# Weight splits made a layer ahead, mean subtractions on GpSimd and an earlier LayerNorm in a two-layer decoder trunk

## The chip, the cores and the metric

The kernel runs on one core of a Trainium2 chip. The metric is the device time of one launch in microseconds, the median of several runs. The profile is of one execution, and its times count from the first instruction of that execution.

## What is computed

The trunk has two layers over 512 tokens of width 1024, all in float32. In each layer the input is RMS-normalised and multiplied by one combined input matrix, whose columns give the branch, the queries of a small attention over 256 memory rows (4 heads of 128) and a gate of width 2048. Layer one's branch is a retention with 8 heads; layer two's is a gated depthwise convolution. The branch and the attention are multiplied by silu(gate), go through an output matrix, are RMS-normalised again and added to the input. The branch of layer two is what the change is about:

```python
u, g, xq, gate = split(proj)          # 1536, 1536, 512, 2048
glu = u * sigmoid(g)
y = causal_depthwise_conv(glu, 31 taps) + dw_b
y = silu(layernorm(y, ln_g, ln_b))    # mean and variance over 1536 channels
```

## The kernel before

**Weights.** The matrices are cut into units of 256 x 512 numbers (512 KB). Each is loaded in float32 by SP (`send`, L159), cast to the matmul's type by ScalarE (`whi`, L181), and the remainder is subtracted by GpSimd in two halves (`wlo`, L188) or by VectorE for some units (L185). A product of activations and weights is then three matmuls, hi x hi, hi x lo and lo x hi (`split3`, L252 to L256). Units 0 to 7 belong to the memory keys and values, 8 to 71 to layer one, 72 on to layer two. When TensorE begins a unit, the one three units on is split (`prefetch`, L193).

**Chunks.** `weave` (L229) writes the program in order: a chunk of six large matmuls, then the side steps due at that place (attention, LayerNorm), then the hooks, then steps of VectorE's list, then products. The order is kept as written on every engine (`manual_schedule`). Layer two is the first projection (32 half chunks), the stages c1, c2, xq, c3, c4, gx, conv5, gate 0, gate 1, gate 2 of 16 chunks each, and the output projection of 64. Per chunk RATE says how many list steps follow and OFFLOAD how many products; what is left over adds up to at most 2.

**The convolution.** The 1536 channels are 12 tiles of 128 x 512, summed in pairs. The list (`tap_sums`, L1084) holds one VectorE multiply-add per tap and tile (`tap_sum`, L1081). `product` (L1050) takes a tap off it: ScalarE multiplies (L1065), GpSimd adds (L1066), only for the pair after the one being summed, once that pair's input tiles are there.

**The LayerNorm.** Once four pairs are summed, LN[0] chunks later, a first mean over eight tiles is taken (`m0_mean`, L1160). It is subtracted from each tile (`shift`, L1151, L1153); the result is squared by ScalarE (L1157) and the squares are added by GpSimd (`gather`, L1131). These moments stand in a second list, `behind`, which every second step serves. `ln_ready` (L1223) empties both lists and treats the last two tiles; `ln_sums` (L1232) lets TensorE sum the squares and the remaining mean; `ln_cols` and `ln_spread` give the inverse deviation. `z_norm` and `z_gate` (L1266, L1274) finish each tile on VectorE and ScalarE and split it for the output projection. LN[1] to LN[4] are the places of these steps, counted from the start of gate 2; the output projection starts at 16.

**The attention** runs beside conv5 and gate 0, by XA: scores (TensorE, VectorE's maxima L505, the negated and scaled maxima L507), exponentials and probabilities (ScalarE, L516, L528), transposes (`p_T`, evacuated by ScalarE at L539 into one of two PSUM buffers' successors), and `av` (L541): TensorE multiplies, VectorE multiplies by the gate (L549), ScalarE casts (L551); two places later VectorE takes the remainder (`yx_lo`, L555).

Of the kernel before, what the change touches and what calls it, by code (L numbers as in the profile page):

```python
# [19 lines left out]
P = 128  # L20
# [71 lines left out]
def trunk(ctx, tc, x, x_t, mem_t, pos, g_cols, w_mem, post_g, w0, w1, dw_w, dw_b,  # L92
# [48 lines left out]
    nc.gpsimd.dma_start(out=inv, in_=c_inv)  # L141
    nc.gpsimd.dma_start(out=zeta, in_=c_zeta)
    nc.gpsimd.dma_start(out=taps, in_=dw_w.rearrange("p (c k) -> p c k", c=NB))
    for i, v in enumerate((dw_b, ln_g, ln_b)):
        nc.gpsimd.dma_start(out=cvec[:, i, :], in_=v)
# [14 lines left out]
    def send(upto):  # L160

        for i in range(sent["dma"], min(upto, sent["conv"] + 3, nu)):
            raws[i] = gp.tile([P, 2, G], F32, tag="wraw", bufs=3, name=nm("wraw"))
# [3 lines left out]
            sent["dma"] = i + 1  # L167

    def conv_units(upto):
        for i in range(sent["conv"], min(upto, nu)):  # L170
            send(i + 1)
            hi = gp.tile([P, 2, G], F32R, tag="whi", bufs=5, name=nm("whi"))
            lo = gp.tile([P, 2, G], F32R, tag="wlo", bufs=5, name=nm("wlo"))
            raw = raws.pop(i)
# [15 lines left out]
            his[i], los[i] = hi, lo  # L190
            sent["conv"] = i + 1
# [276 lines left out]
    def evac_v(a, acc):  # L468
# [9 lines left out]
           (7, conv(4)), (8, lambda: squares("m", mt)), (11, conv(5)), (13, conv(6)),  # L478
# [11 lines left out]
    def xattn(xq, gx, yx, rs=None):  # L490
# [3 lines left out]
        def scores(t):  # L494
            mx, nb = tiny([P, XH]), tiny([P, XH])
            scs = []
            for hp in range(2):
                sc = tp_ps()
                scs.append(sc)
                for j in range(2):  # L500
# [6 lines left out]
                nc.vector.tensor_scalar(out=nb[:, hs], in0=mx[:, hs], scalar1=-1.0,  # L507
                                        scalar2=rs[:, t:t + 1] if rs is not None else SCALE,
                                        op0=ALU.mult, op1=ALU.mult)
            pes[t] = scs, nb  # L510

        def exps(t):
            scs, nb = pes[t]
            pe, sm = w4([P, XH, M]), tiny([P, XH])
            for h in range(XH):
# [25 lines left out]
        def av(t):  # L541
# [9 lines left out]
            nc.scalar.copy(out=yx[0][:, :, tok], in_=g)  # L551
# [157 lines left out]
    with tc.tile_pool(name="l0", bufs=1) as lp:  # L709
# [99 lines left out]
        def x_rstd():  # L809
            rx["c"] = col_rstd([0, 1])  # L810
            rx["s"] = tiny([P, NT])
            nc.gpsimd.tensor_scalar(out=rx["s"], in0=rx["c"], scalar1=SCALE, scalar2=0.0,
                                    op0=ALU.mult, op1=ALU.add)
# [12 lines left out]
        def evac_gx(a, acc):  # L826
# [8 lines left out]
                 (5, x_rstd), (5, mem_diags), (7, x_diags)] + [(c, steps(2)) for c in range(4, 8)])  # L835
        weave(proj(hT, False, evac_copy(xq)), [(0, mem_spread), (1, x_spread)]
# [4 lines left out]
        xa = xattn(xq, gx, yx, rx["s"])({0: (1, 7, 11), 1: (9, 15, 19), 2: (17, 23, 27), 3: (25, 31, 34)})  # L841
# [175 lines left out]
        hT = nxt["get"]  # L1017

# [3 lines left out]
    with tc.tile_pool(name="l1", bufs=1) as lp:  # L1022
# [243 lines left out]
        def z_norm(ct):  # L1266
# [3 lines left out]
            nc.vector.tensor_tensor(out=z, in0=z, in1=ln["rb"], op=ALU.mult)  # L1270
            nc.scalar.activation(out=z, in_=z, func=AF.Silu, scale=cvec[:, 1, ct:ct + 1],
                                 bias=cvec[:, 2, ct:ct + 1])

        def z_gate(ct):  # L1274
            c, j = ct // 4, ct % 4
            z = cy[:, ct, :]
            nc.vector.tensor_tensor(out=z, in0=z, in1=gates[c][j], op=ALU.mult)  # L1277
            if ct in (0, 4):
# [9 lines left out]
        def z_step(ct):  # L1288
            if ct < NB:
                z_norm(ct)  # L1290
            if ct:
                z_gate(ct - 1)

        gate(0, part_of(xa, 1), R[7])
        gate(1, part_of(xa, 2), R[8])
        def norm_of(a, b):

            return [(pos_ - a, fn) for pos_, fn in
                    [(LN[1], ln_ready), (LN[2], ln_sums), (LN[3], ln_cols), (LN[4], ln_spread)]
                    + [(LN[4] + (i + 1) // 2, lambda i=i: z_step(i)) for i in range(NB + 1)]  # L1300
                    if a <= pos_ < b]

        gate(2, norm_of(0, 16), R[9])
# [4 lines left out]
        def yT1(j):  # L1308
            if j >= 4:
# [4 lines left out]
                 norm_of(16, 99))  # L1314
# [65 lines left out]
```

## Time and profile before

| | before |
|---|---|
| median of 3 runs | 830.45 us (830.06 to 831.77) |
| profiled execution: own time, span | 831.9 us, 829.8 us |
| TensorE, VectorE, ScalarE, GpSimd busy | 97%, 63%, 42%, 50% of the span |
| mean granted TensorE clock | 0.99 |
| DMA | 84.97 MB, 102 GB/s over the span |

The span runs from the first to the last instruction of the program; the execution's own time is some 2 us longer. TensorE's busy time is that of pipelined matmuls, so a stretch in which it is busy throughout need not be one at full pace; the number of matmuls in a stretch tells that. DMA-issuing instructions count as idle.

### The profile page before, as it was taken

What the parts mean: (1) busy time and instruction counts of PE and PEld (TensorE: products, weight loads), DVE (VectorE), ACT (ScalarE), POOL (GpSimd) and SP (SyncE); (2) the same over time, 40 slices, a digit from 0 to 9 for tenths busy, and PEclk for the clock granted to TensorE, in tenths of its full rate; (3) what the DMA queues carried; (4) which work ended last, traced back from release to release, by engine and by line L of the source; (5) the groups of instructions that cost most, each with busy time, mean ns of one, the idle gap of its engine ahead of it and who ended that gap; (6) DMA issues with size and microseconds to landing.
All of it is one profiled execution on the core that took longest, in us unless ns stands there. A gap on an engine that the chain in (4) does not pass through costs nothing.

```text
span 829.8 us, 10432 instructions
## 1 busy us (share of the span) xinstructions
PE 806.1 (97%) x3904; PEld 674.9 (81%) x3904; DVE 520.1 (63%) x824; ACT 347.8 (42%) x559; POOL 417.5 (50%) x381
## 2 busy tenths in 40 slices
PE   8999999999999999999999999999999989998896
PEld 7778888888888888888888988888877878766686
DVE  5798112124664641343326489999999999979523
ACT  5754256521111122333325425544578654245511
POOL 3144433346747644100024168998987798356101
PEclk9999999999999999999999999999999999999899
DMA  7733221231222222233522242322312113311612
GB/s 254 267 109 102 102 76 52 77 115 67 74 88 68 73 77 102 87 116 102 203 101 91 89 152 77 103 101 86 106 66 75 51 51 130 121 54 51 226 54 101
DMA packets 24961, 84.97 MB, mean 102 GB/s; under 512 B 2976, under 2 KB 4512, under 8 KB 24656
## 3 DMA queue, kind: packets, MB, share of 16 engines
q1 hardware_dynamic: 24256, 83.90, 29.1%
q8 instruction: 30, 0.49, 0.2%
q10 hardware_dynamic: 432, 0.21, 0.1%
q0 software_dynamic: 224, 0.21, 0.1%
q14 instruction: 19, 0.16, 0.1%
HBM read 80.11 MB, written 4.19 MB: 102 GB/s over the span
## 4 chain that ended last, share of the span: by engine, by line
PE 76%; DVE 14%; ACT 4%; DMA 3%; POOL 1%; issue 1%; SPq 0%; POOLq 0%; DVEq 0%; ACTq 0%
PE mm L254 22%; PE mm L255 22%; PE mm L256 22%; DVE acc L1081 5%; DMA wraw<-in_w_mem 2%; DVE cy L1277 2%; PE acc L921 1%; DVE wlo L185 1%; ACT whi L181 1%; PE tp L545 1%; PE tp L502 1%; DVE cy L1153 1%; PE tp L902 1%; PE acc L923 1%; DVE cy L1270 1%
## 5 line engine op out<-in xcount | busy, mean ns | idle before, releaser
L188 POOL TENSOR_TENSOR wlo<-wraw,whi 128x512 fp32r<-128x512 f32 x184 | 239.1, 1324 | 234.0 <-ACT whi L181 225.1
L254 PE MATMUL mm<-big,whi 128*128 128x512 f32 (+1 forms) x608 | 235.7, 388 | 5.3 <-ACT whi L177 2.6
L256 PE MATMUL mm<-big,wlo 128*128 128x512 f32 (+1 forms) x608 | 228.3, 375 | 0.4 <-DVE wlo L185 0.3
L255 PE MATMUL mm<-big,whi 128*128 128x512 f32 (+1 forms) x608 | 227.9, 375 | 0.0
L1081 DVE SCALAR_TENSOR_TENSOR acc<-gl,taps,acc 128x512 f32<-128x512 f32 x292 | 195.7, 747 | 0.4
L181 ACT CAST whi<-wraw 128x1024 fp32r<-128x1024 f32 x133 | 137.2, 1046 | 88.7 <-PE mm L256 32.7
L256 PE MATMUL mm<-whi,big 128*128 128x512 f32 (+1 forms) x432 | 168.3, 390 | 0.6 <-POOL big L701 0.5
L254 PE MATMUL mm<-whi,big 128*128 128x512 f32 (+1 forms) x408 | 162.6, 398 | 0.0
L255 PE MATMUL mm<-wlo,big 128*128 128x512 f32 (+1 forms) x408 | 157.8, 387 | 0.9 <-DVE wlo L185 0.9
L254 PEld LDWEIGHTS mm<-big,whi 128*128 128x128 f32 x608 | 115.7, 190 | 25.3 <-ACT big L1220 2.8
L256 PEld LDWEIGHTS mm<-big,wlo 128*128 128x128 f32 x608 | 115.5, 190 | 21.5 <-DVE wlo L185 0.5
L255 PEld LDWEIGHTS mm<-big,whi 128*128 128x128 f32 x608 | 115.7, 190 | 18.9 <-issue 0.5
L256 PEld LDWEIGHTS mm<-whi,big 128*128 128x128 f32 x432 | 81.7, 189 | 19.0 <-POOL big L701 2.2
L255 PEld LDWEIGHTS mm<-wlo,big 128*128 128x128 f32 x408 | 76.8, 188 | 16.0 <-DVE wlo L185 1.3
L254 PEld LDWEIGHTS mm<-whi,big 128*128 128x128 f32 x408 | 76.7, 188 | 14.5 <-issue 0.2
L185 DVE TENSOR_TENSOR wlo<-wraw,whi 128x1024 fp32r<-128x1024 f32 x41 | 53.3, 1316 | 41.2 <-ACT whi L181 41.1
L1066 POOL TENSOR_TENSOR part<-part,pr 128x512 f32<-128x512 f32 x56 | 72.6, 1317 | 5.6 <-ACT pr L1065 5.6
L894 ACT ACTIVATE kz<-tp,zeta 128x384 f32<-128x384 f32 x8 | 4.7, 584 | 96.5 <-PE tp L892 96.5
L1065 ACT ACTIVATE pr<-gl,taps 128x512 f32<-128x512 f32 x56 | 38.3, 716 | 0.1
L505 DVE TENSOR_REDUCE tiny<-tp 128x2 f32<-128x512 f32 x16 | 11.0, 684 | 27.0 <-PE tp L502 27.0
L327 POOL TENSOR_SCALAR tiny<-tiny,tiny 128x1 f32<-128x1 f32 x11 | 3.0, 271 | 41.1 <-ACT pr L602 34.6
L1039 ACT ACTIVATE gl<-mm 128x512 f32<-128x512 f32 x12 | 7.2, 599 | 38.5 <-PE mm L256 38.5
(220 smaller groups left out, 885.6 us busy)
## 6 DMA issues: line engine op xcount, KB each, us to landing
wraw<-in_w SPq DMA_DIRECT2D x126, 512.0 KB, 3.3
wraw<-in_w_mem SPq DMA_DIRECT2D x7, 512.0 KB, 5.3
big<-in_x_t SPq DMA_DIRECT2D x2, 1024.0 KB, 7.4
o<-in_x SPq DMA_DIRECT2D x1, 2048.0 KB, 8.7
x1d<-o SPq DMA_DIRECT2D x4, 512.0 KB, 2.7
o<-x1d SPq DMA_DIRECT2D x1, 2048.0 KB, 10.0
out<-o SPq DMA_DIRECT2D x3, 512.0 KB, 2.6
big<-in_mem_t SPq DMA_DIRECT2D x4, 256.0 KB, 7.2
```

The source lines that it names most:

```text
L181: nc.scalar.copy(out=hi, in_=raw)
L185: nc.vector.tensor_tensor(out=lo, in0=raw, in1=hi.bitcast(F32), op=ALU.subtract)
L188: nc.gpsimd.tensor_tensor(out=lo[:, k], in0=raw[:, k], in1=hi[:, k].bitcast(F32), op=ALU.subtract)
L254: nc.tensor.matmul(dst, lh, rh, start=start, stop=False)
L255: nc.tensor.matmul(dst, lh, rl, start=False, stop=False)
L256: nc.tensor.matmul(dst, ll, rh, start=False, stop=stop)
L502: nc.tensor.matmul(sc[:, j * M:(j + 1) * M], xq[:, h, t * P:(t + 1) * P], mkT[:, h, :], start=True, stop=True)
L505: nc.vector.reduce_max(out=mx[:, hs], in_=sc.rearrange("p (a b) -> p a b", a=2), axis=AX.X)
L1065: nc.scalar.activation(out=pr, in_=gl[:, k:k + S], func=AF.Copy, scale=tap)
L1066: nc.gpsimd.tensor_tensor(out=parts[ct], in0=parts[ct], in1=pr, op=ALU.add)
L1081: nc.vector.scalar_tensor_tensor(out=o, in0=gl[:, k:k + S], scalar=tap, in1=ac, op0=ALU.mult, op1=ALU.add)
L1277: nc.vector.tensor_tensor(out=z, in0=z, in1=gates[c][j], op=ALU.mult)
```

## The change

- Eighteen units of layer two (76 to 110, every other one) are split during layer one, half a unit at every sixth chunk: load 256 KB, cast on ScalarE, subtract on GpSimd, store both parts to DRAM. In layer two the two parts are loaded.
- The first-mean subtractions of tiles 0 to 9 go to GpSimd.
- OFFLOAD rises; the LayerNorm steps move forward from the start of the output projection to that of gate 2 (LN counts from gate 0 now), and a tile's steps are spread, two chunks a tile, with its split not before the second chunk of the output projection.
- In the attention the negated maxima are made on ScalarE, and the cast L551 becomes a step of its own one place later.
- Six small constant loads move from GpSimd's queue to SP's, into the first projection.

```diff
-OFFLOAD = (0, 0.3, 0.6, 0.6, 0.6, 0.5, 0.6, 0.9, 0.5, 0, 0.5)
-LN = (7, 17, 19, 21, 24)
+OFFLOAD = (0, 0.4, 0.8, 0.8, 0.8, 0.8, 0.8, 0.9, 0.8, 0.4, 0.5)
+LN = (7, 32, 34, 36, 39)
+PRE = range(76, 112, 2)
...
-    nc.gpsimd.dma_start(out=inv, in_=c_inv)
...
+    def load_small():
+        nc.sync.dma_start(out=inv, in_=c_inv)
+        nc.sync.dma_start(out=zeta, in_=c_zeta)
...
     def conv_units(upto):
...
+            if i in PRE:
+                nc.sync.dma_start(out=hi.bitcast(F32), in_=ahead[i][:, :, 1])
+                nc.sync.dma_start(out=lo.bitcast(F32), in_=ahead[i][:, :, 0])
+                continue
...
+        for n in range(len(todo)):
+            if n:
+                store(n - 1)
+            load(n + 1)
+            st = stage[n]
+            nc.scalar.copy(out=st[:, 1].bitcast(F32R), in_=st[:, 0])
+            nc.gpsimd.tensor_tensor(out=st[:, 0], in0=st[:, 0], in1=st[:, 1], op=ALU.subtract)
+            yield
+        store(len(todo) - 1)
+
+    pace = {"every": 6, "n": 0}
...
-           (7, conv(4)), (8, lambda: squares("m", mt)), (11, conv(5)), (13, conv(6)),
+           (7, conv(4)), (8, lambda: squares("m", mt)), (9, load_small), (11, conv(5)), (13, conv(6)),
...
-                nc.vector.tensor_scalar(out=nb[:, hs], in0=mx[:, hs], scalar1=-1.0,
...
         def exps(t):
...
+            nc.scalar.activation(out=nb, in_=mx, func=AF.Copy,
+                                 scale=rsn[:, t:t + 1] if rs is not None else -SCALE)
...
-            nc.scalar.copy(out=yx[0][:, :, tok], in_=g)
+
+        def yx_hi(t):
+            tok = slice(t * P, (t + 1) * P)
+            nc.scalar.copy(out=yx[0][:, :, tok], in_=gx[:, :, tok])
...
-                        (p, p_T, t, 0.7), (a, av, t, 1.3), (a + 2, yx_lo, t, 0.0)]
+                        (p, p_T, t, 0.7), (a, av, t, 1.3), (a + 1, yx_hi, t, 0.0),
+                        (a + 2, yx_lo, t, 0.0)]
...
+        pace["steps"] = split_ahead(lp)
+        hooks.append(ahead_hook)
...
         def shift(ct):
             z = cy[:, ct, :]
-            nc.vector.tensor_tensor(out=z, in0=z, in1=ln["m0s"], op=ALU.subtract)
+            eng = nc.gpsimd if ct < NB - 2 else nc.vector
+            eng.tensor_tensor(out=z, in0=z, in1=ln["m0s"], op=ALU.subtract)
...
-                    [(LN[1], ln_ready), (LN[2], ln_sums), (LN[3], ln_cols), (LN[4], ln_spread)]
-                    + [(LN[4] + (i + 1) // 2, lambda i=i: z_step(i)) for i in range(NB + 1)]
...
+            steps_ = [(LN[1], ln_ready), (LN[2], ln_sums), (LN[3], ln_cols), (LN[4], ln_spread)]
+            for i in range(NB):
+                at = LN[4] + 1 + 2 * i
+                steps_ += [(at + n, lambda f=f, i=i: f(i)) for n, f in enumerate((z_norm, z_act, z_gate))]
+                steps_.append((max(49 + i, at + 3), lambda i=i: z_split(i)))
+            return [(pos_ - a, fn) for pos_, fn in sorted(steps_, key=lambda s: s[0]) if a <= pos_ < b]
+
+        gate(0, part_of(xa, 1) + norm_of(0, 16), R[7])
+        gate(1, part_of(xa, 2) + norm_of(16, 32), R[8])
+        gate(2, norm_of(32, 48), R[9])
...
+    nc = bacc.Bacc("TRN2", target_bir_lowering=False, num_devices=1,
+                   dynamic_dma_scratch_size=2048)
```

## Rows read from the trace of the kernel before

**Rows 1.** Page, engines: busy us, share of the span, instructions.

```profile
PE 806.1 (97%) x3904; PEld 674.9 (81%) x3904; DVE 520.1 (63%) x824; ACT 347.8 (42%) x559; POOL 417.5 (50%) x381
```

**Rows 2.** Windows, 20 us: PE, PEld, DVE, ACT, POOL busy (x), clock, DMA.

```profile
540.00:560.00 20.00, 20.00 (x90) 16.54 (x89) 19.69 (x31) 9.90 (x14) 20.00 (x17) 1.00 0.29 105
740.00:760.00 20.00, 19.41 (x84) 15.09 (x83) 19.76 (x24) 12.71 (x19) 16.41 (x12) 1.00 0.13 42
760.00:780.00 20.00, 15.11 (x54) 11.47 (x53) 13.91 (x13) 9.68 (x12) 5.98 (x5) 0.83 0.34 112
```

**Rows 3.** Windows by stage: layer one, conv5, gate 0, gate 2; columns likewise.

```profile
60.00:320.00 260.00, 260.00 (x1281) 221.46 (x1280) 112.68 (x244) 82.28 (x134) 137.17 (x118) 1.00 0.24 81
...
604.90:639.90 35.00, 33.26 (x162) 27.28 (x161) 34.72 (x58) 27.71 (x60) 28.59 (x25) 1.00 0.22 76
639.90:673.60 33.70, 30.69 (x163) 25.03 (x161) 33.55 (x49) 24.89 (x44) 25.65 (x18) 1.00 0.14 47
...
697.10:718.90 21.80, 21.80 (x98) 18.02 (x97) 21.80 (x34) 6.48 (x8) 11.41 (x10) 1.00 0.47 167
```

**Rows 4.** Sources: form: ns min/median/max; who sat idle for whom.

```profile
L1153 DVE TENSOR_TENSOR cy<-cy,m x12: 680/1118/1773, 652.4 to 722.5; 128x512 f32<-128x512 f32 x12
...
L1131 POOL TENSOR_TENSOR sum<-sum,pr x8: 1266/1462/1740, 657.9 to 688.3; 128x512 f32<-128x512 f32 x8
...
L1066 POOL TENSOR_TENSOR part<-part,pr x56: 1275/1293/1755, 502.6 to 679.7; 128x512 f32<-128x512 f32 x56
...
  DVE cy L1153: 16.7, 10
```

**Rows 5.** Groups: busy us, mean ns; taps, and GpSimd's weight halves.

```profile
L1081 DVE SCALAR_TENSOR_TENSOR acc<-gl,taps,acc 128x512 f32<-128x512 f32 x292 | 195.7, 747 | 0.4
...
L1081 DVE SCALAR_TENSOR_TENSOR cy<-gl,taps,acc 128x512 f32<-128x512 f32 x12 | 8.4, 739 | 0.0
...
L188 POOL TENSOR_TENSOR wlo<-wraw,whi 128x512 fp32r<-128x512 f32 x184 | 239.1, 1324 | 234.0 <-ACT whi L181 225.1 <-issue 8.8
```

**Rows 6.** Timeline of ScalarE: gate 0's first chunks (start, length).

```profile
645.88 1.04 ACT L181 CAST whi<-wraw 128x1024 fp32r<-128x1024 f32 x1
646.82 1.06 ACT L539 COPY w<-tp 128x512 f32<-128x512 f32 x2
647.77 1.71 ACT L528 ACTIVATE w<-w,tiny 128x256 f32<-128x256 f32 x4
...
650.00 0.58 ACT L1164 ACTIVATE m<-tp 128x512 f32<-128x512 f32 x1
...
653.28 0.64 ACT L1157 ACTIVATE pr<-cy 128x512 f32<-128x512 f32 x1
```

**Rows 7.** Page, DMA issue (us to landing); timeline, one SP issue.

```profile
wraw<-in_w SPq DMA_DIRECT2D x126, 512.0 KB, 3.3
...
2.11 0.43 SPq L399 DMA_DIRECT2D big<-in_mem_t  x1
```

**Rows 8.** Timeline of VectorE, 642 to 652 us.

```profile
642.33 0.17 DVE L507 TENSOR_SCALAR tiny<-tiny 128x2 f32<-128x2 f32 x1
...
647.04 4.67 DVE L1081 SCALAR_TENSOR_TENSOR acc<-gl,taps,acc 128x512 f32<-128x512 f32 x7
651.79 0.69 DVE L549 TENSOR_TENSOR big<-tp,big 128x512 f32<-128x512 f32 x1
```

**Rows 9.** Timeline of TensorE: the chunk behind the variance sums.

```profile
727.65 0.80 PE L254 MATMUL mm<-whi,big 128*128 128x512 f32 x1
```

**Rows 10.** Windows: the stop at 766; first and last of three behind it.

```profile
766.00:768.00 2.00, 0.00 (x0) 0.00 (x0) 1.19 (x2) 1.57 (x4) 0.72 (x2) 1.00 0.00 0
770.00:772.00 2.00, 1.05 (x3) 0.86 (x4) 2.00 (x3) 0.68 (x1) 0.00 (x0) 0.50 0.04 8
...
774.00:776.00 2.00, 2.00 (x6) 1.52 (x6) 0.00 (x0) 0.49 (x1) 0.00 (x0) 0.50 1.00 252
```

More of the change, by code (lines that the diff above doesn't have):

```diff
@@ L140, in trunk @@
     nc.gpsimd.memset(mean_of, 1.0 / BW)
-    nc.gpsimd.dma_start(out=inv, in_=c_inv)
[L142 to L145, printed above, removed]
+    def load_small():
+        nc.sync.dma_start(out=inv, in_=c_inv)
+        nc.sync.dma_start(out=zeta, in_=c_zeta)
+        nc.sync.dma_start(out=taps, in_=dw_w.rearrange("p (c k) -> p c k", c=NB))
+        for i, v in enumerate((dw_b, ln_g, ln_b)):
+            nc.sync.dma_start(out=cvec[:, i, :], in_=v)
     units = [w_mem[i] for i in range(8)]
@@ L173, in conv_units @@
             lo = gp.tile([P, 2, G], F32R, tag="wlo", bufs=5, name=nm("wlo"))
+            his[i], los[i] = hi, lo
+            sent["conv"] = i + 1
+            if i in PRE:
+                nc.sync.dma_start(out=hi.bitcast(F32), in_=ahead[i][:, :, 1])
+                nc.sync.dma_start(out=lo.bitcast(F32), in_=ahead[i][:, :, 0])
+                continue
             raw = raws.pop(i)
@@ L189, in conv_units, with split_ahead, load, store @@
                                             in1=hi[:, k].bitcast(F32), op=ALU.subtract)
-            his[i], los[i] = hi, lo
-            sent["conv"] = i + 1
+    ahead = {i: dp.tile([P, 2, 2, G], F32, name=f"ahead{i}") for i in PRE}
+    def split_ahead(pool):
+        todo = [(i, k) for i in PRE for k in range(2)]
+        stage = {}
+        def load(n):
+            if n < len(todo):
+                i, k = todo[n]
+                stage[n] = pool.tile([P, 2, G], F32, tag="stage", bufs=3, name=nm("stage"))
+                nc.sync.dma_start(out=stage[n][:, 0], in_=units[i][:, k * G:(k + 1) * G])
+        def store(n):
+            i, k = todo[n]
+            nc.sync.dma_start(out=ahead[i][:, k], in_=stage.pop(n))
+        load(0)
+        yield
[6 more added lines that the diff above has]
+            nc.gpsimd.tensor_tensor(out=st[:, 0], in0=st[:, 0], in1=st[:, 1], op=ALU.subtract)
+            yield
+        store(len(todo) - 1)
+    pace = {"every": 6, "n": 0}
+    def ahead_hook():
+        pace["n"] += 1
+        if pace["n"] >= pace["every"]:
+            pace["n"] = 0
+            next(pace["steps"], None)
     def prefetch():
@@ L506, in scores @@
                                      axis=AX.X)
-                nc.vector.tensor_scalar(out=nb[:, hs], in0=mx[:, hs], scalar1=-1.0,
-                                        scalar2=rs[:, t:t + 1] if rs is not None else SCALE,
-                                        op0=ALU.mult, op1=ALU.mult)
-            pes[t] = scs, nb
+            pes[t] = scs, mx, nb
         def exps(t):
-            scs, nb = pes[t]
+            scs, mx, nb = pes[t]
             pe, sm = w4([P, XH, M]), tiny([P, XH])
+            nc.scalar.activation(out=nb, in_=mx, func=AF.Copy,
+                                 scale=rsn[:, t:t + 1] if rs is not None else -SCALE)
             for h in range(XH):
@@ L810, in x_rstd @@
             rx["c"] = col_rstd([0, 1])
-            rx["s"] = tiny([P, NT])
-            nc.gpsimd.tensor_scalar(out=rx["s"], in0=rx["c"], scalar1=SCALE, scalar2=0.0,
-                                    op0=ALU.mult, op1=ALU.add)
+            for key, sc in (("s", SCALE), ("sn", -SCALE)):
+                rx[key] = tiny([P, NT])
+                nc.gpsimd.tensor_scalar(out=rx[key], in0=rx["c"], scalar1=sc, scalar2=0.0,
+                                        op0=ALU.mult, op1=ALU.add)
             for t, acc in late_v:
@@ L1017, in trunk @@
         hT = nxt["get"]
+        hooks.clear()
+        for _ in pace["steps"]:
+            pass
     with tc.tile_pool(name="l1", bufs=1) as lp:
@@ L1277, in z_gate, with z_split @@
             nc.vector.tensor_tensor(out=z, in0=z, in1=gates[c][j], op=ALU.mult)
+        def z_split(ct):
+            c, j = ct // 4, ct % 4
+            z = cy[:, ct, :]
             if ct in (0, 4):
```

21 lines of the change are left out of this document (6 added, 15 removed).

## The prediction

> **What bounds the kernel now.** I read the engines' busy times first. TensorE is busy 97% of the span, VectorE 63%, GpSimd 50% [rows 1]; the sum of the matmuls is fixed by the work, so only the 24 us in which TensorE stands, and the stretches in which it runs slowly, can be won. The windows say where they lie. At full pace 20 us hold 90 large matmuls, as 540 to 560 us does; 740 to 760 holds 84 and 760 to 780 only 54, at a mean granted clock of 0.83 [rows 2]. Those 42 missing matmuls are worth 42 x 0.227 = 9.5 us (0.227 us is a sixth of a chunk, below). The stages come next: layer one from 60 to 320 us has no stop at all, gate 0 of layer two takes 33.7 us with TensorE busy 30.7, and the undisturbed gate 2 takes 21.8 us for its 16 chunks, that is 1.36 us a chunk and 0.227 a matmul [rows 3]. In every one of the gate stages VectorE is busy without a break. So layer two's second half is a race between TensorE and VectorE's list of taps, subtractions and LayerNorm steps, and the change rearranges that list. Each engine works its instructions strictly in the order in which they are written: in gate 0 ScalarE's squares sit behind VectorE's mean subtractions for 16.7 us in all [rows 4].
>
> **Counting the written order.** I number layer two's chunks from 1: 32 half chunks of the first projection, then 16 a stage, so gate 0 is 145 to 160, gate 1 161 to 176, gate 2 177 to 192, the output projection 193 to 256. Working the pace rule (RATE and OFFLOAD added per chunk, products only for the pair of tiles after the one being summed) through for the kernel before gives 304 multiply-adds and 56 products, as the rows have [rows 4, 5]. With the new numbers it gives 290 and 70: the sum of OFFLOAD x 16 rises by 30, but products wait for tiles that are not there yet, and only 14 more are issued. The mean of the first eight tiles then comes after chunk 145 instead of 148; the ten subtractions fall at 145 (one), 146 (two), 147 (one), 149 (three), 150 (one) and 158, 159 (the two late ones); and at the new place of ln_ready, chunk 177, twelve taps are still unspent and are poured out at once.
>
> **Parts with little in them.** The 36 half units in layer one cost ScalarE 36 x 0.53 = 19 us (two copies take 1.06 [rows 6]) and GpSimd 36 x 1.3 = 47 us over some 390 us. From 60 to 320 us ScalarE is busy 82 of 260 us and GpSimd 137 [rows 3], and an eviction is wanted three chunks (4.1 us) after it is issued; I take 0. A gain is excluded where TensorE never stands; if every copy held an eviction it would be 19 us. In layer two 18 units lose a cast of 1.04 us and two GpSimd halves of 1.32 [rows 5, 6], 48 us of GpSimd, which pays for the products and subtractions there. Their loads are issued three units (16 us) ahead, and a 512 KB load lands in 3.3 us [rows 7]: 0. Six small loads leave GpSimd's queue for SP's, where an issue takes 0.43 us [rows 7]: between -1 (the first weights come sooner, with GpSimd's loads out of their way; an estimate of mine below the 0.43 x 6) and +2.6 us if the weights behind them wait for all six; I take 0. The negated maximum leaves VectorE (0.17 us each [rows 8]) for ScalarE, where it stands in front of exponentials that waited for VectorE anyway: 0, at most 16 x 0.17 = 2.7 us won.
>
> **The chain that I expect to decide.** Moved to GpSimd, a subtraction is followed on the same queue by the addition of its own square: subtract (GpSimd), square (ScalarE), add (GpSimd), subtract the next. Each round trip is serial, and GpSimd's queue also holds the products. The price of a GpSimd step: its product sums have a median of 1.29 us, the additions of squares 1.46, up to 1.74 [rows 4]. The long ones ran beside VectorE's subtractions, which themselves reached 1.77 us against 0.68 at best [rows 4]; with the subtractions gone from VectorE I take 1.27, and keep 1.74 as the upper end.
> The Trainium skill (GPSIMD Engine Reference, Key points) says that GpSimd shares its SBUF interfaces with VectorE and contends with instructions of two SBUF inputs; the multiply-adds read one operand from PSUM, so by that rule the low price holds, while by the median of the additions themselves the sum would come out 15 x 0.19 = 2.9 us later. The same page of the Trainium skill (Engine selection) puts two-input elementwise work on VectorE, GpSimd being about twice as slow; the trace has 0.68 at best against 1.27 here, 1.9 times.
> Step by step, on the clock of the trace of before:
> - ScalarE reaches the new place of the mean, right behind chunk 145's cast, at 646.9; its copy takes 0.6 [rows 6]: mean ready 647.5.
> - Up to subtraction 6 GpSimd does 7 subtractions, 5 additions and 3 product sums (chunks 146 to 148): 15 x 1.27 = 19.1. Five squares lie open between them, 0.64 [rows 6] and two hand-overs, 0.05 each by my estimate: 3.7. The first open square stands behind the chunk's copies and probabilities on ScalarE [rows 6]: about 2. Sum 24.8: 672.3.
> - Square 6, a product, and the copy yx_hi of token block 1 (position 5 of gate 0, now after the squares): 0.6 each, 674.2.
> - VectorE reaches yx_lo of that block, chunk 151, after the product at 651.8 [rows 8], four taps later: 655.2. It waits for yx_hi until 674.3, that is 19 us, with all its taps queued behind.
> - TensorE: the PSUM buffer of attention block 2 is freed by copies behind square 7, about 678; at 1.36 us a chunk and its attention matmuls it is there at 665. It stands some 13 us, but what it loses here it would lose later anyway.
> - VectorE's rest up to the variance sums: 67 taps and 2 copies at 0.667 (seven taps 4.67 us [rows 8]) 46.0; five attention steps at 0.69 3.5; two subtractions at 1.11 [rows 4] 2.2; two additions at 0.69 1.4. Sum 53.1: 727.4. The tenth product sum, at about 690, does not hold it further.
> - TensorE, free again at 678, is at the variance sums (three chunks into gate 2) near 714, and stands about 13 us until 727.4. The mean matmul takes 0.6: chunk 180 starts at 728.0.
>
> Now against before: there the chunk behind the variance sums starts at 727.65 [rows 9], but that is chunk 197, 17 chunks further on. So the end moves by 0.3 + 17 x 1.36 = 23.4 us. Back come the 9.5 us of the first part [rows 2]: the LayerNorm tiles (three VectorE steps each, 36 us for twelve) start some 20 chunks before they are needed, and that wait is hidden; were it not, 9.5 us come back. Against that, after the stop at 766 the granted clock was 0.50, 1.2 instead of 2.4 GHz, in the windows from 770 to 776 [rows 10], three of them: half of 6 us lost. The new long stop is nearest to that one: +3.0. Sum: 23.4 - 9.5 + 3.0 = **+16.9 us**. The profiled execution's own time is 831.9 against a median of 830.45; I add the difference to the median: **847.4 us**.
>
> **The rivals.**
> *The chain does not hold VectorE* (not slower): if the squares' round trips finished before VectorE comes to yx_lo at 655.2, everything behind moves up by the 19.1 us: 828.3, with the same bounds 826 to 833. For it: GpSimd has 48 us less splitting. Against it: 15 steps cannot be done in the 7.7 us between the mean and yx_lo; it needs the mean some 19 us earlier, and ScalarE is not free for it. The point from which it decides is a hold of 17 us: below that the kernel is no slower. Chance 0.15, of which 0.09 faster and 0.06 the same.
> *The LayerNorm tiles are late again* (slower still): they start only at about 740, and if they are as slow as the 3 us each of now and the splits queue on GpSimd, 9.5 us are not won: 856.9. Against it: first wanted at chunk 205, last at 225. Chance 0.06.
> *Layer one pays*: 36 copies hold evictions or their stores hold SP's queue: up to 19 us, 858 to 866. Against it: TensorE's unbroken 260 us there [rows 3]. Chance 0.04.
> *My chain*: 0.75. Its own range: +7.1 with GpSimd at 1.74 and +2.6 at the start, so 857; down 1.7 for TensorE's idle time in the stage before gate 0 (35.0 long, 33.3 busy [rows 3]) and 2.7 for the maxima: 843.
>
> **The numbers.** The likeliest case gives 847.4. The range 834 to 858 leaves out the unheld case and layer one's, 0.19. A measurement of this kernel can tell about 0.2% from no change, 1.7 us; faster by more 0.09, within 0.06, slower 0.85.
>
> **What would show it.** Right: 290 multiply-adds, 70 products; VectorE idle near 655 to 674 waiting for ScalarE's yx copy; ScalarE's squares waiting for GpSimd; TensorE standing over 10 us at attention block 2 in gate 0 and again at the variance sums in gate 2; no stop among the LayerNorm tiles; layer one as before. Wrong: if VectorE runs through gate 0 without that hole, or if the variance sums come before 715.

## The result, and the profile after

The changed kernel takes **853.15 us** (median of 4 runs, 852.90 to 853.39) against 830.97 us for the kernel before, measured beside it (4 runs, 830.06 to 831.77): a ratio of 1.0267, 95% interval 1.0249 to 1.0285. It is 22.2 us slower. Forecast were 847.4 us and a range of 834 to 858.

In the lines below, some numbers have moved: the multiply-adds are L1138 (before L1081), the subtractions L1211 (L1153), the squares L1215 (L1157), their sums L1186 and L1188 (L1129, L1131), the products and their sums L1122 and L1123 (L1065, L1066), the copies yx hi and yx lo L601 and L605, the attention's transposes, their copies and the multiplication behind them L585, L586 and L592, the variance sums L1293 and L1294, a gate tile's eviction L1278, the maxima of the scores L553 (L505), VectorE's copy of a pair's product sum L1131 (L1074), the weights' casts and remainders L192 and L199 (L181, L188), a chunk's three matmuls L302 to L304 (L254 to L256). In some of the experiments the later lines are a few numbers further on: the variance sums are L1299 or L1296 there, the eviction L1284, the additions of squares L1218.

The engines of the changed kernel (busy us, share of the span, instructions), to be set against [rows 1]:

```profile
PE 806.8 (95%) x3904; PEld 677.3 (80%) x3904; DVE 493.5 (58%) x784; ACT 359.0 (42%) x599; POOL 446.1 (52%) x400
```

TensorE does the same work in a span that is 21.3 us longer, VectorE does 27 us less, GpSimd 29 us more. So no engine became the bound by its sum; time went into waiting. The windows (busy us and instructions of PE, PEld, DVE, ACT and POOL, then the granted clock, the DMA share and GB/s) say where:

```profile
60.00:320.00 260.00, 260.00 (x1280) 221.43 (x1280) 112.47 (x236) 96.14 (x161) 166.28 (x142) 1.00 0.46 150
600.00:640.00 40.00, 35.97 (x164) 30.36 (x163) 34.23 (x56) 25.75 (x60) 23.25 (x21) 0.91 0.25 81
640.00:680.00 40.00, 24.85 (x123) 19.89 (x121) 14.42 (x24) 18.49 (x38) 23.78 (x19) 0.90 0.23 79
680.00:720.00 40.00, 34.90 (x161) 29.07 (x162) 36.76 (x56) 19.07 (x28) 30.38 (x25) 0.93 0.19 66
720.00:740.00 20.00, 11.60 (x40) 5.82 (x39) 16.92 (x27) 3.72 (x5) 4.80 (x4) 0.83 0.08 27
760.00:780.00 20.00, 20.00 (x89) 16.54 (x89) 13.60 (x21) 14.25 (x20) 20.00 (x15) 1.00 0.20 66
```

Layer one from 60 to 320 us is as full as before [rows 3], with the 36 half units in it. The stretch from 760 to 780 us, which held 54 matmuls [rows 2], now holds 89. The loss lies between 600 and 740 us, and TensorE's largest waits (in total, times, longest) name three places:

```profile
PE tp L592 <- ACT w L586: 15.4, 1, 15.4
PE acc L1293 <- DVE cy L1138: 8.3, 1, 8.3
PE tp L592 <- DVE acc L1138: 4.0, 1, 4.0
```

The first is attention block 2 in gate 0, the second the variance sums in gate 2, both of which were forecast; the third lies in conv5 and was not.

The chain itself, in the timelines of the changed kernel (start, duration, engine, line, operation, idle time before it and what ended it); first GpSimd and ScalarE:

```profile
649.78 0.61 ACT L1222 ACTIVATE m<-tp 128x512 f32<-128x512 f32 x1
649.97 2.53 POOL L199 TENSOR_TENSOR wlo<-wraw,whi 128x512 fp32r<-128x512 f32 x2 [19.28 <-ACT whi L192]
652.45 2.55 POOL L1211 TENSOR_TENSOR cy<-cy,m 128x512 f32<-128x512 f32 x2
...
672.28 1.26 POOL L1211 TENSOR_TENSOR cy<-cy,m 128x512 f32<-128x512 f32 x1
673.58 0.63 ACT L1215 ACTIVATE pr<-cy 128x512 f32<-128x512 f32 x1 [2.59 <-POOL cy L1211]
674.28 1.26 POOL L1188 TENSOR_TENSOR sum<-sum,pr 128x512 f32<-128x512 f32 x1 [0.74 <-ACT pr L1215]
675.50 1.26 POOL L1211 TENSOR_TENSOR cy<-cy,m 128x512 f32<-128x512 f32 x1
676.79 0.63 ACT L1215 ACTIVATE pr<-cy 128x512 f32<-128x512 f32 x1 [2.59 <-POOL cy L1211]
677.94 0.60 ACT L601 CAST big<-big 128x512 fp32r<-128x512 f32 x1
```

Then VectorE and TensorE, which stand behind it:

```profile
678.58 0.74 DVE L605 TENSOR_TENSOR big<-big,big 128x512 fp32r<-128x512 f32 x1 [18.86 <-ACT big L601]
682.85 3.38 PE L592 MATMUL tp<-w,mv 128*128 128x128 f32 x16 [15.42 <-ACT w L586]
701.48 28.40 DVE L1138 SCALAR_TENSOR_TENSOR acc<-gl,taps,acc 128x512 f32<-128x512 f32 x43
730.58 1.86 PE L1293 MATMUL acc<-sum,ones 128*1 128x512 f32 x2 [8.35 <-DVE cy L1138]
735.33 0.79 PE L302 MATMUL mm<-big,whi 128*128 128x512 f32 x1
```

One round is read from the three rows at 672.28 to 674.28: GpSimd subtracts (1.26), ScalarE squares (0.63) while GpSimd stands 0.74 us, GpSimd adds (1.26). So the two hand-overs take 0.11 us (0.74 less 0.63). ScalarE stands 2.59 us for the next tile, and with it yx hi, for which VectorE stands 18.86 us. What TensorE waits for at block 2 are the copies of its probabilities (L586), which the multiplication L592 reads and which lie behind the next square. Later 43 taps run without a break up to the variance sums; TensorE has to wait for them.

The third place, in VectorE's timeline of conv5:

```profile
624.32 0.69 DVE L1131 COPY acc<-part 128x512 f32<-128x512 f32 x1 [1.60 <-POOL part L1123]
628.04 0.69 DVE L1131 COPY acc<-part 128x512 f32<-128x512 f32 x1 [2.23 <-POOL part L1123]
629.44 1.28 DVE L553 TENSOR_REDUCE tiny<-tp 128x2 f32<-128x512 f32 x2
```

At the start of a pair VectorE takes over GpSimd's sum of the products that were already made for it. Before, it came to this pair at 635.46 us; now it comes 13 us sooner, mostly because more products in the earlier stages make its list shorter (some 3 us of it are left when the old OFFLOAD is put back, see below), while conv5 (OFFLOAD 0.9 in both kernels) is still issuing products for that very pair. GpSimd has the last one behind a weight split:

```profile
624.25 2.52 POOL L199 TENSOR_TENSOR wlo<-wraw,whi 128x512 fp32r<-128x512 f32 x2
626.72 1.29 POOL L1123 TENSOR_TENSOR part<-part,pr 128x512 f32<-128x512 f32 x1
```

VectorE stands 1.60 and 2.23 us for them, with the scores' maxima written behind its copies.

### The profile page after: what moved, and what is told of

It reads as the page before. It is cut to its first block, busy times and chain, and to the rows that moved or that the text cites. A ratio compares the mean times of both kernels' runs of the same rounds, so it can differ in the third digit from the quotient of the medians.

```text
span 851.1 us, 10660 instructions
## 1 busy us (share of the span) xinstructions
PE 806.8 (95%) x3904; PEld 677.3 (80%) x3904; DVE 493.5 (58%) x784; ACT 359.0 (42%) x599; POOL 446.1 (52%) x400
## 2 busy tenths in 40 slices
DMA packets 43171, 122.74 MB, mean 144 GB/s; under 512 B 4976, under 2 KB 6640, under 8 KB 42864
## 4 chain that ended last, share of the span: by engine, by line
PE 78%; DVE 9%; ACT 5%; POOL 5%; issue 2%; DMA 1%; POOLq 0%; DVEq 0%; ACTq 0%
PE mm L302 22%; PE mm L303 22%; PE mm L304 22%; DVE acc L1138 6%; POOL part L1123 2%; POOL cy L1211 1%; PE tp L592 1%; PE acc L975 1%; PE tp L550 1%; PE tp L956 1%; PE acc L977 1%; POOL sum L1188 1%; PE acc L302 1%; PE acc L303 1%; PE acc L304 1%
## 5 line engine op out<-in xcount | busy, mean ns | idle before, releaser
L199 POOL TENSOR_TENSOR wlo<-wraw,whi 128x512 fp32r<-128x512 f32 x148 | 192.1, 1322 | 150.6 <-ACT whi L192 147.4
L302 PE MATMUL mm<-big,whi 128*128 128x512 f32 (+1 forms) x608 | 237.1, 390 | 4.4 <-ACT big L1278 2.3
L304 PE MATMUL mm<-big,wlo 128*128 128x512 f32 (+1 forms) x608 | 228.3, 376 | 0.0
L1138 DVE SCALAR_TENSOR_TENSOR acc<-gl,taps,acc 128x512 f32<-128x512 f32 x278 | 185.9, 750 | 0.4
L304 PE MATMUL mm<-whi,big 128*128 128x512 f32 (+1 forms) x432 | 166.9, 386 | 0.0
L302 PE MATMUL mm<-whi,big 128*128 128x512 f32 (+1 forms) x408 | 162.0, 397 | 0.0
L302 PEld LDWEIGHTS mm<-big,whi 128*128 128x128 f32 x608 | 115.9, 191 | 25.1 <-ACT big L1278 3.1
L192 ACT CAST whi<-wraw 128x1024 fp32r<-128x1024 f32 x115 | 119.4, 1047 | 39.0 <-PE mm L304 14.2
L304 PEld LDWEIGHTS mm<-big,wlo 128*128 128x128 f32 x608 | 115.7, 190 | 20.9 <-DVE wlo L189 0.2
L229 POOL TENSOR_TENSOR stage<-stage 128x512 f32<-128x512 f32 x36 | 49.2, 1366 | 92.8 <-ACT stage L228 92.8
L304 PEld LDWEIGHTS mm<-whi,big 128*128 128x128 f32 x432 | 81.1, 188 | 16.9
L1123 POOL TENSOR_TENSOR part<-part,pr 128x512 f32<-128x512 f32 x70 | 89.6, 1313 | 9.3 <-ACT pr L1122 9.2
L302 PEld LDWEIGHTS mm<-whi,big 128*128 128x128 f32 x408 | 76.7, 188 | 14.5
L196 DVE TENSOR_TENSOR wlo<-wraw,whi 128x1024 fp32r<-128x1024 f32 x41 | 56.5, 1388 | 43.9 <-ACT whi L192 41.6
L1122 ACT ACTIVATE pr<-gl,taps 128x512 f32<-128x512 f32 x70 | 47.2, 717 | 5.3 <-POOL part L1123 5.3
L228 ACT CAST stage<-stage 128x512 fp32r<-128x512 f32 x36 | 22.3, 620 | 50.3 <-DMA stage<-in_w 29.5
L592 PE MATMUL tp<-w,mv 128*128 128x128 f32 x128 | 18.8, 310 | 19.5 <-ACT w L586 15.4
```

What stands on the lines that cost most here:

```text
L199: nc.gpsimd.tensor_tensor(out=lo[:, k], in0=raw[:, k], in1=hi[:, k].bitcast(F32), op=ALU.subtract)
L228: nc.scalar.copy(out=st[:, 1].bitcast(F32R), in_=st[:, 0])
L229: nc.gpsimd.tensor_tensor(out=st[:, 0], in0=st[:, 0], in1=st[:, 1], op=ALU.subtract)
L302: nc.tensor.matmul(dst, lh, rh, start=start, stop=False)
L304: nc.tensor.matmul(dst, ll, rh, start=False, stop=stop)
L592: nc.tensor.matmul(po[:, h * P:(h + 1) * P], mv[:, m, h * P:(h + 1) * P], pT[:, m, h, :], start=m == 0, stop=m == 1)
```

## The experiments

The theory to be tested had three parts in series: the chain of serial rounds in gate 0, the variance sums that VectorE's list can't reach in time, and (new, from the trace after) the late product sums in conv5. Ratios are to the kernel before.

### The subtractions on VectorE again

```diff
-            eng = nc.gpsimd if ct < NB - 2 else nc.vector
+            eng = nc.vector
```

> The changed kernel with one part undone: the ten first-mean subtractions are VectorE's again. Chain theory (in gate 0 ScalarE's yx copy waits behind squares, they wait for GpSimd's subtract and add trips, and VectorE loses 18.9 us behind that copy): the hole goes, ten subtractions of about 1.05 us come back to VectorE, so the end is 8 to 10 us earlier, 843 to 846, and TensorE still stops at the variance sums. Rival, early LayerNorm (the cost is that the lists are emptied at the start of gate 2 with twelve taps unspent, whoever subtracts): within 2 us of 853.

Measured 840.86 us, ratio 1.0125 (1.0109 to 1.0142): 12.3 less than the changed kernel, 2 more than the theory gave. The stop of 15.4 us is gone from TensorE's waits, and VectorE's idle time before yx lo fell from 25.8 to 5.7 us in all. What is left:

```profile
PE acc L1293 <- DVE cy L1138: 8.2, 1, 8.2
PE mm L302 <- ACT big L1278: 4.3, 2, 2.8
PE tp L592 <- DVE acc L1138: 4.0, 1, 4.0
```

The subtractions on GpSimd made the hole. But the kernel is still slower than the one before: the stop at the variance sums and that in conv5 are untouched by this edit.

### The LayerNorm steps eight chunks later

```diff
-LN = (7, 32, 34, 36, 39)
+LN = (7, 40, 42, 44, 47)
```

> The changed kernel with the LayerNorm steps eight chunks later (LN 7, 40, 42, 44, 47), subtractions still on GpSimd. Chain theory: VectorE's hole in gate 0 stays over 15 us; eight chunks are 10.9 us, more than TensorE's stop of 8.3 us at the variance sums, which goes together with the slow clock behind it: 842 to 845. Rival, early LayerNorm: this alone brings the kernel back to 831 or below.

Measured 842.48 us, ratio 1.0145 (1.0130 to 1.0160): 10.7 less. The stop at the variance sums is gone, that at attention block 2 stays at 15.4, and no new one is among the LayerNorm tiles.

### Both

> Both edits: subtractions on VectorE and LayerNorm eight chunks later. Chain theory: they remove different things, so they add: 8 to 10 from the first, 10 to 11 from the second, 832 to 836. Rival, early LayerNorm: the same time as with the later LayerNorm alone, within 2 us.

Measured 829.09 us, ratio 0.9981 (0.9969 to 0.9993), 3 us below the expected range. The two gains, 12.3 and 10.7, add up to 23.0, and together they gave 24.1. So the two stops lie in series, and each costs its own time.

### The old offload

```diff
-OFFLOAD = (0, 0.4, 0.8, 0.8, 0.8, 0.8, 0.8, 0.9, 0.8, 0.4, 0.5)
+OFFLOAD = (0, 0.3, 0.6, 0.6, 0.6, 0.5, 0.6, 0.9, 0.5, 0, 0.5)
```

> The changed kernel with OFFLOAD of before: 14 products fewer, 14 multiply-adds (9.3 us) more on VectorE. Rival, too many products on GpSimd: the kernel gets over 10 us faster, below 843. Chain theory: GpSimd's chain in gate 0 is shorter by about three product sums (4 us) and the wait for product sums in conv5 (4 us) goes, the multiply-adds come back: 848 to 857.

Measured 850.23 us, ratio 1.0241 (1.0225 to 1.0256), 2.9 less. The stop in conv5 is gone, since VectorE comes to that pair's copy only at 632.58 us. The stop at attention block 2 is gone too (0.3 us), but not the chain: VectorE's hole lies one block later, and TensorE stands 10.6 us at a gate tile's eviction, which is written on ScalarE behind the last squares of the chain. With fewer products VectorE has more taps, and the stop at the variance sums grew from 8.3 to 17.2 us:

```profile
PE acc L1293 <- DVE cy L1138: 17.2, 1, 17.2
PE mm L302 <- ACT big L1278: 10.6, 1, 10.6
682.60 0.69 DVE L605 TENSOR_TENSOR big<-big,big 128x512 fp32r<-128x512 f32 x1 [13.73 <-ACT big L601]
```

From the first subtraction to the start of the eighth it is 26.2 us here, with two product sums and a weight split among them, and 28.0 in the changed kernel, with four product sums. So fewer products hardly shorten the chain, and they lengthen VectorE's list. Which copy stands behind the chain decides where it is paid.

### The kernel before with the splits ahead alone

The kernel before, with the 36 half units in layer one, their loads in layer two and the six small loads on SP; nothing else of the change.

> The kernel before with the splits ahead and the moved small loads alone: order of the mean, subtractions, squares, probabilities and LayerNorm tiles as before. Chain theory: layer one hides the 36 half units and their stores, so nothing of the 22.7 us lies there: 829 to 832 us, TensorE without a new stop from 60 to 320 us, and GpSimd's 48 us of halves missing in layer two without an effect, because there the queue was not last. Rival 'layer one pays': 835 us or more, with evictions waiting for ScalarE before 320 us. Second rival, a freer GpSimd queue already shortens gate 0 of layer two (squares, yx): 825 us or less.

Measured 829.07 us, ratio 0.9976 (0.9967 to 0.9984). The window over layer one shows the same 1280 matmuls and no idle time, with a DMA share nearly twice the former one:

```profile
60.00:320.00 260.00, 260.00 (x1280) 221.43 (x1279) 114.61 (x244) 94.83 (x157) 166.37 (x142) 1.00 0.45 150
```

So this part is worth 1.7 us of gain and none of the loss.

### Each square added after the next subtraction

```diff
-                gather("dsum", square(ct))
+                sq = square(ct)
+                if "late" in ln:
+                    gather("dsum", ln.pop("late"))
+                if ct in (NM - 1, NM + 1):
+                    gather("dsum", sq)
+                else:
+                    ln["late"] = sq
```

> The changed kernel with one edit: GpSimd adds each square only after it has issued the next subtraction, so that ScalarE's square runs beside it. Chain theory: the five hand-overs of some 0.74 us that GpSimd stands for are hidden, and one addition of 1.27 us moves behind the yx copy: some 5 us less, 846 to 850 us; VectorE's hole at yx_lo shrinks from 18.9 to 13 to 15 us, and the stop at the variance sums shrinks too. Rival, GpSimd's sheer number of steps holds the queue, and the round trips cost nothing: 852 us or more. Rival, the subtractions do not matter at all and the hole comes from elsewhere: hole unchanged.

Measured 846.19 us, ratio 1.0181 (1.0168 to 1.0194): 7.0 less, at the near end of what was expected. VectorE's hole before yx lo and TensorE's stops:

```profile
673.75 1.35 DVE L605 TENSOR_TENSOR big<-big,big 128x512 fp32r<-128x512 f32 x1 [13.52 <-ACT big L601]
PE tp L592 <- ACT w L586: 9.4, 1, 9.4
PE acc L1299 <- DVE cy L1138: 8.8, 1, 8.8
```

The hole shrank by 5.3 us and the stop at block 2 by 6.0. A part of the price was the order alone; the stop at the variance sums did not shrink, which had been expected too.

### Fewer products in conv5, alone

```diff
-OFFLOAD = (0, 0.4, 0.8, 0.8, 0.8, 0.8, 0.8, 0.9, 0.8, 0.4, 0.5)
+OFFLOAD = (0, 0.4, 0.8, 0.8, 0.8, 0.8, 0.8, 0.5, 0.8, 0.4, 0.5)
```

> The changed kernel with the share of the products in conv block 5 at 0.5 instead of 0.9, and nothing else. The prediction did not have the stop there (4.0 us on TensorE and its low clock). Theory: this wait moves everything behind it, the mean too, so without it the time is the one that the chain alone gives: 853.2 less 4 to 6, so 847 to 849.5 us. Rival, the chain in gate 0 absorbs it (VectorE and TensorE wait there anyway, so an earlier start only makes a longer wait): 851.5 us or more, and the stop at attention block 2 grows by the 4 us.

Measured 847.19 us, ratio 1.0194 (1.0180 to 1.0208): 6.0 less. VectorE comes to the pair at nearly the same time (623.25 us, against 622.7) and finds the sum done. Gate 0 does not absorb it; the whole of it moves up by 5.6 us, with the hole and the stop as long as they were, and only the stop at the variance sums grows, from 8.35 to 9.66 us:

```profile
673.02 0.74 DVE L605 TENSOR_TENSOR big<-big,big 128x512 fp32r<-128x512 f32 x1 [18.87 <-ACT big L601]
677.29 3.47 PE L592 MATMUL tp<-w,mv 128*128 128x128 f32 x16 [15.43 <-ACT w L586]
724.32 1.87 PE L1293 MATMUL acc<-sum,ones 128*1 128x512 f32 x2 [9.66 <-DVE cy L1138]
729.50 0.79 PE L302 MATMUL mm<-big,whi 128*128 128x512 f32 x1
```

### The copy yx hi on VectorE

```diff
-            nc.scalar.copy(out=yx[0][:, :, tok], in_=gx[:, :, tok])
+            nc.vector.tensor_copy(out=yx[0][:, :, tok], in_=gx[:, :, tok])
```

> The changed kernel with one link of the chain taken out: the copy yx hi is made by VectorE instead of ScalarE, so that yx lo no longer waits for ScalarE; subtractions and squares stay as they are. Chain theory: VectorE's hole of 18.9 us at yx lo goes, but the probabilities of attention block 2 are still copied by ScalarE behind the squares, so TensorE's stop of 15.4 us stays and VectorE comes to stand at the product of that block, some eleven taps (7 to 8 us) further on. The stop at the variance sums (8.3 us) all but goes: 843 to 847 us. Rival, the yx copy was the only link that mattered: both stops go, 838 us or less. Rival, TensorE's stop at attention block 2 decides all of it: 851 us or more.

Measured 851.73 us, ratio 1.0255 (1.0239 to 1.0271): only 1.4 less, and the two intervals overlap. The theory's 843 to 847 us is missed; what came is the last rival, that the stop at block 2 decides. The stop at the variance sums, expected to all but go, is 6.5 us. The hole moved as expected, eleven taps further, but it was hardly shorter:

```profile
661.89 7.33 DVE L1138 SCALAR_TENSOR_TENSOR acc<-gl,taps,acc 128x512 f32<-128x512 f32 x11
685.97 0.69 DVE L596 TENSOR_TENSOR big<-tp,big 128x512 f32<-128x512 f32 x1 [16.75 <-PE tp L592]
682.15 3.78 PE L592 MATMUL tp<-w,mv 128*128 128x128 f32 x16 [14.82 <-ACT w L586]
```

In the changed kernel VectorE did those eleven taps from 679.24 on and came to the product of block 2 at 686.48; here it comes to it at 685.97. In the changed kernel the taps had lain beside the end of TensorE's wait and its product for block 2. ScalarE holds VectorE by two links of nearly equal length, yx hi of block 1 and the probabilities of block 2; taking out the one that ended the wait leaves the other.

### Two versions without the stops

With the subtractions on VectorE, conv5's share at 0.5 (the text on record says that it goes back to that; it was 0.9 before too) and LN = (9, 41, 43, 45, 48):

> The changed kernel with all subtractions on VectorE, the share of the products in conv block 5 back from 0.9 to 0.5, and the LayerNorm steps 2 and 8 to 9 chunks later (9, 41, 43, 45, 48). Chain theory: no chain is left, and the stop in conv block 5 (4.1 us on TensorE and its half clock), which came from VectorE waiting for GpSimd's product sums, goes as well: 829.1 less 4 to 6, so 822 to 826 us, faster than both kernels. Rival, the LayerNorm tiles start too late and TensorE waits in the output projection: 829 us or more, with stops at matmuls that wait for yh or yl tiles. Rival, conv block 5's stop has another cause: it stays at about 4 us, and the time at 828 to 830.

Measured **822.61 us**, ratio 0.9901 (0.9887 to 0.9915): faster than both kernels, and as forecast. One stop of 4.3 us is left, where a gate tile's eviction lies on ScalarE behind the square of tile 8, for which VectorE has not yet subtracted the mean:

```profile
678.92 0.79 PE L302 MATMUL mm<-big,whi 128*128 128x512 f32 x1 [4.26 <-ACT big L1278]
```

With the subtractions on GpSimd, but LN = (14, 41, 43, 45, 48), the list `behind` served every third step, each square added later as above, and the OFFLOAD of before:

> The subtractions stay on GpSimd as in the changed kernel, but paced: mean at 14 instead of 7, a step every third turn, additions behind the next subtraction, the products of the kernel before (fewer), variance sums at chunk 41. Chain theory, where the fault is that a chain of serial hand-overs is packed in front of the yx copy and not GpSimd as such: most of the 24 us come back, 820 to 831 us, with no hole over 3 us at yx_lo. Rival, GpSimd's steps take so long (1.3 us and more against 0.7) that wherever they stand they hold ScalarE and VectorE: 836 us or more, with the hole moved to a later copy or to the variance sums.

Measured 825.38 us, ratio 0.9925 (0.9912 to 0.9937). GpSimd can carry the subtractions; the hole at yx lo is 3.3 us, a little over the 3 expected. But TensorE stands 4.95 us at a gate tile's eviction, which lies on ScalarE behind squares that wait for GpSimd:

```profile
674.97 1.34 DVE L605 TENSOR_TENSOR big<-big,big 128x512 fp32r<-128x512 f32 x1 [3.32 <-ACT big L601]
697.41 0.80 PE L302 MATMUL mm<-big,whi 128*128 128x512 f32 x1 [4.95 <-ACT big L1284]
```

A stop of that kind stands in the version with VectorE's subtractions too. So most of the cost in the changed kernel came from where the subtractions stand, all in front of yx hi, and from the order of the additions, and not from the engine by itself. Since this version changes four settings at once, which of them does how much stays open.

### Two attempts at the last stop

To the version of 822.61 us, the squares of tiles 8 and later went to GpSimd:

```diff
-            nc.scalar.activation(out=sq, in_=cy[:, ct, :], func=AF.Square)
+            if ct < NM:
+                nc.scalar.activation(out=sq, in_=cy[:, ct, :], func=AF.Square)
+            else:
+                nc.gpsimd.tensor_tensor(out=sq, in0=cy[:, ct, :], in1=cy[:, ct, :], op=ALU.mult)
```

> The last version (subtractions on VectorE, conv block 5's products halved, LayerNorm steps at 9, 41, 43, 45, 48) with one more edit: the squares of the two late tiles (8 and 9) on GpSimd instead of ScalarE. In that version TensorE still stood 4.3 us at 674.7 us, because a gate tile's eviction lay on ScalarE behind the square of tile 8, which waited for VectorE's subtraction. Theory (one queue holding another): the stop and the half clock behind it go, 822.6 less 4 to 6, so 816.5 to 819 us. Rival, VectorE's list is late by itself and the stop only moves to the variance sums or to the yx tiles: 821 us or more.

Measured 825.89 us, ratio 0.9939 (0.9927 to 0.9952), slower than without it. The stop of 4.3 us is gone, and 4.79 and 1.50 stand at the variance sums instead:

```profile
712.95 1.86 PE L1296 MATMUL acc<-sum,ones 128*1 128x512 f32 x2 [4.79 <-DVE cy L1138]
716.31 3.57 PE L1296 MATMUL acc<-pr,ones 128*1 128x512 f32 x4 [1.50 <-POOL pr L1218]
```

VectorE's last taps end at 713.5 us here and at 714.2 us in the version before it: its list is the limit, and without its stop TensorE only comes to the variance sums too early. So the variance sums were moved three chunks back (44, 46, 48, 51), and the squares of tiles 10 and 11 back to ScalarE:

> The version with the late squares on GpSimd, now for tiles 8 and 9 alone (the squares of tiles 10 and 11 are ScalarE's again), and its four LayerNorm steps three chunks later (44, 46, 48, 51). There VectorE poured out its last 43 taps without a break up to 713.5 us and TensorE stood 4.8 and 1.5 us for it at the variance sums. Theory: VectorE's list sets the time of the variance sums, and three chunks of matmuls (4.1 us) written ahead of them are won, with the 1.5 us of GpSimd's two squares: 825.9 less 5 to 7, so 819 to 821 us. Rival, the LayerNorm tiles now come too late for the output projection and TensorE waits there instead: 823 us or more.

Measured 827.27 us, ratio 0.9954 (0.9941 to 0.9968): not the gain that was expected, and the rival's range. Whether it is slower than the version before it can't be told: the intervals overlap, and the kernel before, run beside each, was 831.87 us here and 830.87 there. The waits of 4.79 and 1.50 us shrank to 0.7 and 0.9 (two edits at once, the place and two of the squares, so not all of it is the place's), but now TensorE waits for the split LayerNorm tiles (`yh` and `big`) in the output projection, by about half a microsecond at a time and 1.18 once:

```profile
766.13 0.50 PE L302 MATMUL mm<-whi,yh 128*128 128x512 f32 x1 [1.18 <-ACT yh L751]
760.00:780.00 20.00, 17.73 (x68) 13.44 (x67) 12.11 (x16) 9.82 (x16) 5.34 (x5) 0.91 0.26 91
```

The window from 760 to 780 us holds 68 matmuls and a clock of 0.91, between the 54 and 0.83 of the kernel before [rows 2] and the 89 of the changed one. That is the wait of the kernel before, coming back. In this version no place tried is without a wait: three chunks earlier TensorE waits for VectorE's list, and here it waits a little for the list and already for the tiles.

## Why the prediction was right, and where its sizes were off

**Mechanism and sign.** Step by step, the third column being the run with fewer products in conv5, in which the part that I had not seen is taken out:

| step | forecast | changed kernel | without conv5's wait |
|---|---|---|---|
| multiply-adds, products | 290, 70 | 290, 70 | 293, 67 |
| mean ready | 647.5 | 650.4 | 644.8 |
| GpSimd's mean step | 1.27 | 1.28 (subtractions) | |
| yx hi of block 1 done | 674.2 | 678.5 | 673.0 |
| VectorE's hold at yx lo | 19 | 18.9 | 18.9 |
| TensorE's stop at block 2 | 13 | 15.4 | 15.4 |
| VectorE's list done | 727.4 | 733.7 | 727.5 |
| TensorE's stop at the variance sums | 13 | 8.3 | 9.7 |
| chunk 180 starts | 728.0 | 735.3 | 729.5 |
| from there to the end | 118.7 | 115.8 | 115.8 |

(A done time is the start plus the duration of the row; 733.7 is VectorE's last addition ahead of the variance sums, 733.02 + 0.69, the 727.5 likewise. The last row's forecast is what the sum implies: 829.8 - 727.65, and 23.1 for 17 chunks, less 9.5, plus 3.0.)

**The step that failed** is "counting the written order". It gave the number of products, 70, and no more: I did not carry it on to the place where VectorE takes over a pair's sum. That place moved 13 us forward, into the stage that is still making products for the pair, and VectorE waits there, with the maxima of the scores and all of the attention behind it. For conv5 I had only a possible gain (1.7 us of TensorE's idle time there). The wait is worth 6.0 us by the run with fewer products, and with it the forecast sum would have been 853.4. That this is so near the measured 853.15 is partly luck, and so is the nearness of 847.19, the run without the wait, to my 847.4: there chunk 180 starts 1.5 us after my time, and the rest is 2.9 us shorter than my sum for it.

**Two terms that offset each other.** Ahead of the first subtraction GpSimd had two halves of a weight split (2.53 us at 649.97), so the chain starts 2.1 us after the mean is ready, which I had not counted; without conv5's wait the mean is ready 2.7 us before my time for it. From the first subtraction to the start of the square that I called 6 (the seventh) it then takes 24.3 us in both runs (652.45 to 676.79); my sum for it was 24.8. My price of 1.27 for a GpSimd step held, but the reason that I gave is hardly tested there: beside most of these steps VectorE ran no multiply-adds, it stood in its hole. TensorE's 13 us at the variance sums came out shorter because TensorE arrives at 722.2 and not near 714: it left block 2 4.9 us later, and needed 39 us from there and not 36. Since it waits there in any case, that does not show in the sum.

**The clock.** I added 3.0 us behind chunk 180. The granted clock did fall to 0.53 from 680 to 686 us and to 0.54 from 728 to 734:

```profile
680.00:686.00 6.00, 3.15 (x17) 3.15 (x17) 6.00 (x10) 4.30 (x8) 4.95 (x5) 0.53 0.00 0
728.00:734.00 6.00, 3.37 (x5) 0.38 (x6) 5.67 (x9) 1.23 (x2) 0.00 (x0) 0.54 0.00 0
734.00:740.00 6.00, 6.00 (x26) 3.93 (x25) 3.24 (x6) 2.48 (x3) 2.46 (x2) 1.00 0.01 3
```

But the first of these lies ahead of a stop in which TensorE waits for VectorE anyway, and the second on the variance sums themselves; from 734 us on it was 1.00 (2.4 GHz). The term is the 2.9 us by which the last row of the table is shorter. Half speed ahead of a wait cost nothing here. The second stretch did cost something, ahead of chunk 180: the four matmuls of the squares take 2.34 us (1.88 in the kernel before), and the chunk starts 1.6 us after VectorE's list is done, 2.0 in the run without conv5's wait, where I had 0.6.

**The terms at nothing.** Layer one at 0: right, 260 of 260 us busy. The small loads and the splits in layer two at 0: the two together gained 1.7 us. The negated maxima at 0 had a wrong price: I took 0.17 us each from one row, and the six ahead of that pair in the kernel before take 0.17 to 1.10 us, 3.5 in all, near the 2.9 us by which VectorE comes to conv5's pair sooner with the old OFFLOAD (632.58 against 635.46). No run has them alone. The LayerNorm tiles' 9.5 us back: right, 89 matmuls where 54 were, and no stop.

**The rivals.** For the case in which the chain does not hold VectorE I had 828.3 us. The run with the subtractions on VectorE takes the hold away, and gives 840.9. Its 12.5 us over my figure are, to within 2 us, the stop at the variance sums (8.2) and conv5's wait (6.0): I had let both go with the hold. VectorE's list is too long for variance sums at their early place with or without the hold: when TensorE no longer stands in gate 0, it comes to them sooner too (at 709.9 instead of 722.2 us). Layer one paying, and the LayerNorm tiles late again, did not occur.

**The balance.** Three stops, taken away one at a time: 12.3, 10.7 and 6.0, in all 29.0. The change cost 22.2, so if the three simply add, the rest of it gained some 7. The version in which all three are gone is 8.2 us faster than the kernel before, run beside it (830.77 to 822.61), which fits. The splits ahead and the small loads are 1.7 of it; how the rest divides between the LayerNorm tiles' earlier start and VectorE's shorter list was not tried.

## What to carry to other kernels

When a step moves to another engine, write down each round trip that it makes there (here GpSimd, ScalarE, GpSimd, with 0.74 us of standing in each), and then look at what is next in line on *both* queues; what pays is the unrelated copy behind the last of them. Removing the stop that a trace names may only uncover a second one of the same length (yx hi and the probabilities) or the next in series (the variance sums), so price a rival after recounting who then arrives early. And a step that may be written anywhere has a window: too early it waits for its producer, too late its consumer waits for it; in the last two versions the variance sums at place 43 (counted in chunks from gate 0) still had to wait for VectorE's list, and with those at place 46 the LayerNorm tiles came late.

## What the runs showed of the hardware

In the changed kernel GpSimd's subtractions took 1.26 to 1.30 us, 1.28 on average over ten. Six of them ran while VectorE stood idle, three beside nothing but its multiply-adds, which read one operand from PSUM (1.29, 1.26 and 1.28), so the multiply-adds cost them nothing. Beside yx lo, which reads two tiles in SBUF, a product sum took 1.72:

```profile
678.72 1.72 POOL L1123 TENSOR_TENSOR part<-part,pr 128x512 f32<-128x512 f32 x1
```

VectorE's own subtractions of two SBUF tiles, put back, took between 0.68 and 1.75 us. The three with no GpSimd instruction beside them took 0.68 to 0.69, and the longest ran beside two product sums, as these rows of that run show:

```profile
654.32 0.68 DVE L1211 TENSOR_TENSOR cy<-cy,m 128x512 f32<-128x512 f32 x1
679.24 1.75 DVE L1211 TENSOR_TENSOR cy<-cy,m 128x512 f32<-128x512 f32 x1
677.48 5.88 POOL L1123 TENSOR_TENSOR part<-part,pr 128x512 f32<-128x512 f32 x4
```

The Trainium skill (GPSIMD Engine Reference, Key points) says that the two engines share their SBUF interfaces and contend at instructions with two SBUF inputs; these rows agree with it: both engines' steps grew where VectorE's had two SBUF inputs, and GpSimd's did not beside the multiply-adds.

The DMA traffic grew from 84.97 to 122.74 MB and its share over layer one from 0.24 to 0.46 without one idle microsecond of TensorE there. I had expected no cost, but not that so much more traffic would leave no mark.
